# Two hybrid layers on one core: retention as full-array matmuls with zero-padded operands, the sum of the merged branches in SBUF, and longer times in the planner's yields

## The chip, the cores and the metric

The kernel runs on one core of a Trainium2 chip. The metric is the device time of one execution in microseconds (us). Five engines work side by side, each through its own instructions in order: PE (TensorE, matrix products), DVE (VectorE), ACT (ScalarE), POOL (GpSimd) and SP (SyncE, which here issues most of the DMA transfers). An instruction that needs the result of another engine waits, and whatever stands behind it on its engine waits with it. PE's clock has two levels, 1.2 and 2.4 GHz; the column PEclk of the profile is the granted clock as a share of the full one.

## The reference

Two blocks follow one another on a sequence of 512 positions of width 1024, in float32. The first (a gated recurrent mixer, a gated spatial mixer and a feed-forward part) is not touched. The second is two layers of this form:

```python
h = _rms(x) * norm1_g
proj = h @ w_in
aq, ak, av, rw, rq, rk, rv, rg, gates = _split(proj, IN_SIZES)
...
o_a = sliding_window_attention(aq, ak, av, attn_sinks) @ w_attn_o
o_b = rwkv7_time_mix(rw, ...) @ w_rwkv_o
o_c = retention(rq, rk, rv, rg) @ w_ret_o
g = jax.nn.sigmoid(gates).reshape(B, T, N_BRANCH, D)
mixed = g[:, :, 0] * o_a + g[:, :, 1] * o_b + g[:, :, 2] * o_c
x = x + mixed @ w_out
```

and then a feed-forward part with a residual. Each branch has 8 heads of 64 numbers. Retention goes over chunks of 128 positions, and carries a 64x64 state per head from one to the next:

```python
s = jnp.einsum('bnihd,bnjhd->bnhij', qc, kc) * dmat
inner = jnp.einsum('bnhij,bnjhe->bnihe', s, vc)
kv = jnp.einsum('bnjhd,bnjhe,hj->bnhde', kc, vc, zeta)
def step(R, kv_n):
    return R * chunk_decay[None, :, None, None] + kv_n, R
_, r_prev = lax.scan(step, jnp.zeros((B, H, d, d), jnp.float32), kv)
cross = jnp.einsum('bnihd,nbhde,hi->bnihe', qc, r_prev, xi)
```

## The kernel before

**Layout.** An activation is kept transposed: 8 tiles of 128 channels (partitions) by 512 positions. P is 128, T is 512, KT is 8.

**Dense products.** Each big product runs as three matmuls of 128x128 by 128x512 on the two halves (high and low) of both operands. The weights come in blocks. SP loads two blocks with one DMA of 512 KB (`raw`, line 89), ACT casts the high half of a block (`hl`, line 101), POOL subtracts it to get the low half (line 212, `hl<-raw,hl`), and PE works off 12 matmuls per block (line 151). Four `hl` buffers let ACT and POOL be up to three blocks ahead of PE. The products end in PSUM tiles `psd` (three), those of the small chains in `psr` (two pairs) and `psm` (one).

**A layer of the second block** (`layer`) has these stages, with their times in the profiled execution for the first and the second layer:
- the rwkv stage, 1060 to 1385 and 2100 to 2430 us: two chains `rwkv_pair`, of two head pairs each, with dense products in between;
- the attention stage, 1385 to about 1558 and 2430 to about 2602 us: two chains `attn_block` and the chain `ret` (retention), again with dense products in between;
- the rest of the dense products, to 1662 and 2705 us. They end with `projections(0)`, 8 blocks that multiply the attention output by `w_attn_o`;
- the `w_ret_o` stage, 8 blocks, to 1674 and 2717 us, and then `w_out` and the feed-forward part.

**What sets the order.** On PE the order of the program is kept (`manual_schedule`), and the function `weave` writes it. A chain is a generator. It issues its instructions up to a `yield` with a number: an estimate, in us of PE work, of how long the other engines need until the chain can go on. Until that much PE work (by the kernel's own counter `self.pe`) has been issued, `weave` takes steps of the other chains, or else of the dense products (`fmg`, three matmuls per step). A larger number therefore puts more dense matmuls between two parts of a chain. The order on the other engines and DMA queues is set by a scheduler, from the dependences and its own priorities.

**The sum of the branches.** Each of the three projections multiplies its product by a gate (`s`, loaded from DRAM into a tile `ld`; the DVE operation is on line 227) and adds it to a running sum. The sum lies in eight DRAM tiles `accd`. `projections(1)` stores it (`acc<-ld`). `projections(0)` and the `w_ret_o` stage load it (`ld<-acc`), add on DVE (line 212, `ld<-ld,ld`) and, in `projections(0)`, store it again.

**Retention** (`ret`). A chunk holds q and k as four tiles of two heads (64 partitions each). Scores take the 64 rows of one head as a 64x128 operand (in the profile `x,x`); the product with v is written in two halves of 64 output rows (`v,rs`), the product with the carried state `rr` in two halves of 64x64 (`rr,qx`).

**Names in the rwkv chain.** `AR,BK` are the two score groups of a pair, `SC` the masked scores that DVE makes of them; `kp` is a working tile (`wt`) that is copied from PSUM on line 1537, and `Zb` a tile whose copy from PSUM line 1513 makes and which a DMA (`solve`) rearranges.

## Time and profile before

| | us |
|---|---|
| median of three runs | 3144.87 |
| lowest, highest | 3140.88, 3152.83 |
| profiled execution | 3142.22 |
| its span | 3140.1 |
| PE busy | 2987.4 (95%) |
| mean granted clock of PE | 0.979 |

The span runs from the first to the last instruction of the core; 2.1 us of the execution lie around it. PE is busy for 95% of it, DVE for 47%, POOL for 44% and ACT for 36%.

### The profile page before, as it was taken

To read this page: it belongs to the slowest core of one execution; us is meant where nothing else is said; L and a number is where in the kernel's file an instruction comes from. 1 tells how busy PE (TensorE), PEld (TensorE's weight loads), DVE (VectorE), ACT (ScalarE), POOL (GpSimd) and SP (SyncE) were. 2 spreads that over 40 slices of the span, in tenths; PEclk is the share of its full clock that TensorE was granted. 3 is DMA by queue.
4 is the path that set the end of the run, shared out by engine and by line. 5 is a ranking of instruction groups with operands and counts; after the bars stand their busy time and mean duration, and the time that the engine had idled before them with its cause. 6 is when DMAs were issued, how large, how long until landed. Compare 5 with 4: busy or idle time off the path is not lost. (4 is left out here: it accounts for less than half of the span.)

```text
span 3140.1 us, 48643 instructions
## 1 busy us (share of the span) xinstructions
PE 2987.4 (95%) x19104; PEld 2406.1 (77%) x19104; DVE 1464.9 (47%) x2870; ACT 1120.9 (36%) x2059; POOL 1389.2 (44%) x1117
## 2 busy tenths in 40 slices
PE   6999999889999989998999999999999999999999
PEld 5787887678888767786777888877778778778887
DVE  6765457662324776636424222228574552432121
ACT  3544422243232433334423322334332453333232
POOL 3442444434444433242345555564233324465453
PEclk9999999999999999998999999999999999999999
DMA  5221346423333443342465323334333336632333
GB/s 205 75 80 56 108 141 225 170 68 97 98 94 98 136 111 96 94 132 86 141 202 174 101 93 95 100 132 127 91 100 118 112 95 186 227 99 92 97 94 94
DMA packets 206819, 372.32 MB, mean 119 GB/s; under 512 B 71040, under 2 KB 107136, under 8 KB 203520
## 3 DMA queue, kind: packets, MB, share of 16 engines
q1 hardware_dynamic: 185152, 365.78, 37.2%
q10 hardware_dynamic: 21440, 3.45, 0.6%
q8 instruction: 150, 2.46, 0.3%
q14 instruction: 77, 0.63, 0.1%
HBM read 323.02 MB, written 46.14 MB: 118 GB/s over the span
## 5 line engine op out<-in xcount | busy, mean ns | idle before, releaser
L212 POOL TENSOR_TENSOR hl<-raw,hl 128x512 fp32r<-128x512 f32 (+2 forms) x924 | 1194.6, 1297 | 1584.2 <-ACT hl L101 1442.7
L151 PE MATMUL psd<-u,hl 128*128 128x512 f32 (+1 forms) x7176 | 1720.2, 396 | 16.2 <-ACT u L231 3.5
L151 PEld LDWEIGHTS psd<-u,hl 128*128 128x128 f32 x7176 | 1334.1, 192 | 310.1 <-issue 12.1
L101 ACT CAST hl<-raw 128x512 fp32r<-128x512 f32 (+2 forms) x924 | 554.4, 604 | 1221.4 <-PE psd L151 934.6
L151 PE MATMUL psd<-hf,hl 128*128 128x512 f32 x1056 | 248.8, 396 | 0.0
L151 PEld LDWEIGHTS psd<-hf,hl 128*128 128x128 f32 x1056 | 197.8, 188 | 47.4
L151 PE MATMUL psd<-hl,hl 128*128 128x512 f32 x576 | 142.3, 406 | 13.3 <-DVE ld L227 13.3
L151 PEld LDWEIGHTS psd<-hl,hl 128*128 128x128 f32 x576 | 110.5, 194 | 43.5 <-issue 9.2
L212 DVE TENSOR_TENSOR s<-psd,rstd 128x512 f32<-128x512 f32 x88 | 60.5, 691 | 177.1 <-PE psd L151 153.7
L212 DVE TENSOR_TENSOR x<-x,psd 128x512 f32<-128x512 f32 x48 | 33.0, 687 | 235.9 <-PE psd L151 235.9
L227 DVE SCALAR_TENSOR_TENSOR hf<-s,hf 128x512 fp32r<-128x512 f32 x66 | 53.9, 817 | 155.7 <-ACT hf L139 155.5
L212 DVE TENSOR_TENSOR z<-psd,rstd 128x512 f32<-128x512 f32 x80 | 55.0, 688 | 137.3 <-PE psd L151 137.1
L151 PE MATMUL psd<-hl,u 128*128 128x512 f32 (+1 forms) x480 | 104.5, 366 | 2.2 <-DVE zq L227 1.9
L227 DVE SCALAR_TENSOR_TENSOR acc<-wada,cond,acc 128x256 f32<-128x256 f32 x152 | 99.3, 678 | 2.4
L212 DVE TENSOR_TENSOR raw<-raw,rows 128x512 f32<-128x512 f32 x60 | 57.5, 998 | 84.4 <-DMA raw<-in_wst 84.4
L151 PEld LDWEIGHTS psd<-hl,u 128*128 128x128 f32 x480 | 81.5, 190 | 18.3 <-DVE zq L227 2.0
L151 PE MATMUL psd<-mix,hl 128*128 128x512 f32 x384 | 89.4, 393 | 1.3 <-DVE ld L227 1.2
L139 ACT ACTIVATE hf<-s 128x512 fp32r<-128x512 f32 x66 | 41.7, 632 | 127.5 <-POOL s L212 116.7
L151 PEld LDWEIGHTS psd<-mix,hl 128*128 128x128 f32 x384 | 71.8, 188 | 18.7 <-DVE ld L227 3.0
L227 DVE SCALAR_TENSOR_TENSOR nt<-nt,nt 128x8 f32<-128x8 f32 (+3 forms) x330 | 78.6, 242 | 8.0
L227 DVE SCALAR_TENSOR_TENSOR s<-s,s 128x512 f32<-128x512 f32 x44 | 55.9, 1270 | 28.2 <-ACT s L139 28.0
L151 PE MATMUL psr<-hl,hf 128*128 128x512 f32 x264 | 66.9, 390 | 0.6 <-POOL hl L212 0.5
(374 smaller groups left out, 3230.7 us busy)
## 6 DMA issues: line engine op xcount, KB each, us to landing
raw<-in_wst SPq DMA_DIRECT2D x390, 512.0 KB, 3.6
wada<-in_wada SPq DMA_DIRECT2D x24, 1024.0 KB, 6.1
raw<-in_wst SPq DMA_DIRECT2D x32, 448.0 KB, 3.2
raw<-in_wst SPq DMA_DIRECT2D x32, 384.0 KB, 3.0
gd<-z SPq DMA_DIRECT2D x48, 256.0 KB, 4.2
ld<-gd SPq DMA_DIRECT2D x48, 256.0 KB, 3.9
acc<-ld SPq DMA_DIRECT2D x32, 256.0 KB, 3.5
ld<-acc SPq DMA_DIRECT2D x32, 256.0 KB, 3.7
```

Of the source, the lines that this page charges most:

```text
L101: self.nc.scalar.copy(h[:, 0, :w], t)
L139: return self.nc.scalar.activation(out, in_, getattr(AF, func), **k)
L151: return self.nc.tensor.matmul(out, lhsT, rhs, start=start, stop=stop, **k)
L212: return (eng or self.nc.vector).tensor_tensor(out, a, b, op=op)
L227: return self.nc.vector.scalar_tensor_tensor(out, a, s, b, op0=op0, op1=op1, **k)
```

## The change

**The sum of the branches.** `acc` is now one SBUF tile of 128 x 8 x 512, and the DRAM tiles are gone with their 32 stores and 32 loads of 256 KB. `projections(1)` writes `acc` with its DVE operation. `projections(0)` adds into it on POOL. The `w_ret_o` stage multiplies by the gate and adds `acc`, both on DVE.

**Retention.** Two tiles `qz` hold q with the other head's 64 partitions at zero; two tiles `rz` hold the carried state in the same way, and take turns over the chunks. Scores take all 128 rows of k and `qz`; the products with v and with the state are each one matmul with 128 columns of weights in place of two with 64. The state's update is two DVE multiplications of 64 partitions in place of one of 128. Per chunk ACT makes two copies of 64x512 into `qz`.

**Attention.** k is zero-padded in the same way, and its scores take all 128 rows. The loads of the mask and of the sinks stand earlier in the program.

**The planner.** Eight numbers in yields are larger, and the copy into `kp` goes from DVE to ACT.

```diff
         self.xd = [dt(f"xd{m}", [P, T]) for m in range(KT)]
-        self.accd = [dt(f"acc{m}", [P, T]) for m in range(KT)]
         self.gd = [[dt(f"gd{b}{m}", [P, T]) for m in range(KT)] for b in range(3)]
...
         return s
-
-    def merged(self, l, s, name, m, xs):
-
-        py = yield from self.fmg(name, l, range(m * P, (m + 1) * P), xs)
-        self.stt(s, s, 1.0, py, OP.add, OP.mult)
...
                     s = from_memory(self.gd[br][m])
+                    py = yield from self.fmg("w_rwkv_o_2" if br else "w_attn_o_2", l, range(m * P, (m + 1) * P), xs)
+                    o = acc[:, m] if br else s
+                    self.stt(o, s, 1.0, py, OP.add, OP.mult)
                     if br == 0:
-                        ld = from_memory(self.accd[m])
-                    yield from self.merged(l, s, "w_rwkv_o_2" if br else "w_attn_o_2", m, xs)
-                    if br == 0:
-                        self.add(s, s, ld)
-                    nc.sync.dma_start(self.accd[m], s)
+                        self.add(acc[:, m], acc[:, m], s, nc.gpsimd)
                     yield
...
             ahl, chl = new4(HP.pool, "a"), new4(HP.pool, "c")
+            acc = HP.pool.tile([P, KT, T], F, name=self.n("acc"), tag="acc")
             at = {}
...
             for m in range(KT):
-                s, ld = from_memory(self.gd[2][m]), from_memory(self.accd[m])
-                self.run(self.merged(l, s, "w_ret_o_2", m, cs))
-                self.add(s, s, ld)
+                s = from_memory(self.gd[2][m])
+                self.stt(s, s, 1.0, self.fm("w_ret_o_2", l, range(m * P, (m + 1) * P), cs), OP.add, OP.mult)
+                self.add(s, s, acc[:, m])
                 self.split_half(mix[m][:, 0], mix[m][:, 1], s)
...
         q = yp.tile([P, 4, T], F, name=self.n("q"), tag="yq")
-        k = yp.tile([P, T], F, name=self.n("k"), tag="yk")
+        k = yp.tile([P, 2, T], F, name=self.n("k"), tag="yk")
+        nc.gpsimd.memset(k, 0.0)
+        sw = self.cload(yp, "swmask")
+        sink = yp.tile([P, 8], F, name=self.n("sink"), tag="sink")
+        nc.sync.dma_start(sink, self.a["attn_sinks_2"][l:l + 1, :].broadcast_to((P, 8)))
         sq = yp.tile([P, 4, 10], F, name=self.n("sq"), tag="ysq")
...
         self.tm("w_in_2", l, range(I_AK, I_AK + 256), self.us, donek)
-        yield 7.0
+        yield 8.5
         r = self.rsqrt(yp, "ya", sq.rearrange("p t h -> p (t h)"), 1.0 / 64, RMS_EPS).rearrange("p (t h) -> p t h", h=10)
...
             self.tr(ps[:, t * P:(t + 1) * P], zk[:, t])
-        self.act(k, ps, "Copy", scale=self.v2("k_norm", l))
+        for kv in range(2):
+            h = slice(64 * kv, 64 * kv + 64)
+            self.act(k[h, kv], ps[h], "Copy", scale=self.v2("k_norm", l)[h])
         yield 1.0
...
             yield 0.8
-        sw = self.cload(yp, "swmask")
-        sink = yp.tile([P, 8], F, name=self.n("sink"), tag="sink")
-        nc.sync.dma_start(sink, self.a["attn_sinks_2"][l:l + 1, :].broadcast_to((P, 8)))
         env.update(q=q, k=k, vt=vt, sw=sw, sink=sink)
...
             for i in range(2):
-                self.mm(ps[:, i * 256:i * 256 + w], q[r, 2 * g + i, c], k[r, k0:k0 + w])
+                self.mm(ps[:, i * 256:i * 256 + w], q[:, 2 * g + i, c], k[:, kv, k0:k0 + w])
             self.add(s[:, 2 * g:2 * g + 2, :w], ps.rearrange("p (i s) -> p i s", s=256)[:, :, :w],
...
             self.act(s[:, h, :w], s[:, h, :w], "Copy", scale=mx[:, 3, h:h + 1])
-        yield 8.5
+        yield 10.0
         pt = yp.tile([P, 8, P], F, name=self.n("pt"), tag=f"ypt{kv}")
...
         x3 = xi.rearrange("p (j i) -> p j i", i=P)
-        r1 = None
-        bc = lambda t, n: t.rearrange("p (h o) -> p h o", o=1).broadcast_to((P, t.shape[1], n))
+
+        qz = [cp.tile([P, 4, P], F, name=self.n("qz"), tag=f"qz{e}") for e in range(2)]
+        rz = [cp.tile([P, 2, 4, 64], F, name=self.n("rz"), tag=f"rz{i}") for i in range(2)]
+        for t in qz + rz:
+            nc.gpsimd.memset(t, 0.0)
+        bc = lambda t, n: t.rearrange("p (h o) -> p h o", o=1).broadcast_to((t.shape[0], t.shape[1], n))
         for n in range(4):
...
             nc.sync.dma_start(g, self.rd["g"].rearrange("j p t -> p j t")[:, :, c])
-            r0 = r1
+            r0, r1 = rz[(n + 1) % 2], rz[n % 2]
             if n:
...
                 self.mul(kz, ps.rearrange("p (h d) -> p h d", d=64), bc(zeta, 64))
+            for e in range(2):
+                r = slice(64 * e, 64 * e + 64)
+                nc.scalar.copy(qz[e][r], q[r])
             yield 1.5
...
             for e in range(2):
-                r = slice(64 * e, 64 * e + 64)
                 ps = self.psum("r1")
                 for j in range(4):
-                    self.mm(ps[:, j * P:(j + 1) * P], k[r, j], q[r, j])
+                    self.mm(ps[:, j * P:(j + 1) * P], k[:, j], qz[e][:, j])
                 s.append(cp.tile([P, 4, P], F, name=self.n("rs"), tag=f"rs{e}"))
...
             for e in range(2):
-                r = slice(64 * e, 64 * e + 64)
                 po = self.psum("r1")
                 for j in range(4):
-                    for h in (slice(0, 64), slice(64, 128)):
-                        self.mm(po[h, j * 64:(j + 1) * 64], s[e][:, j, h], v[:, (2 * j + e) * 64:(2 * j + e) * 64 + 64], True, n == 0)
-                    for h in (slice(0, 64), slice(64, 128)) if n else ():
-                        self.mm(po[h, j * 64:(j + 1) * 64], qx[r, j, h], r0[r, j], False, True)
+                    self.mm(po[:, j * 64:(j + 1) * 64], s[e][:, j], v[:, (2 * j + e) * 64:(2 * j + e) * 64 + 64], True, n == 0)
+                    if n:
+                        self.mm(po[:, j * 64:(j + 1) * 64], qx[:, j], r0[:, e, j], False, True)
                 nc.scalar.copy(o[:, :, e], po[:, :256].rearrange("p (j d) -> p j d", d=64))
...
                     self.mm(ps[:, j * P:(j + 1) * P], kz[:, 2 * j:2 * j + 2].rearrange("p h d -> p (h d)"), v[:, j * P:(j + 1) * P])
-                r1 = cp.tile([P, 4, 64], F, name=self.n("rr"), tag="rr", bufs=2)
                 kv = ps.rearrange("p (j e d) -> p j e d", e=2, d=64)
-                if n:
-                    self.mul(r1, r0, bc(cd, 64))
                 for e in range(2):
...
                     if n:
-                        self.add(r1[r], r1[r], kv[r, :, e])
+                        self.mul(r1[r, e], r0[r, e], bc(cd[r], 64))
+                        self.add(r1[r, e], r1[r, e], kv[r, :, e])
                     else:
-                        nc.vector.tensor_copy(r1[r], kv[r, :, e])
+                        nc.vector.tensor_copy(r1[r, e], kv[r, :, e])
             o8 = o.rearrange("p j e d -> p (j e) d")
...
             self.mul(o8, o8, bc(rs, 64))
-            yield 10.5
+            yield 12.0
             ps = self.psum("r1")
...
         for h in range(2):
-            yield 2.2 if h else 11.0
+            yield 2.5 if h else 13.0
             pss = [psum() for _ in ER]
...
-        yield 1.9
+        yield 4.5
         UV = [tl(f"z{e}", (P, NC, 64)) for e in range(2)]
...
         wt = tl("kp", (P, NC, 64))
-        nc.vector.tensor_copy(wt, each(of(M1), of(xd)))
-        yield 1.4
+        nc.scalar.copy(wt, each(of(M1), of(xd)))
+        yield 2.0
         p2, p1 = each(of(zd), of(wt)), each(of(wt), of(zd))
...
         self.add(zd, p1, zd)
```

**The order in three places.** First PE in the first layer, third head pair: from the last matmul of its second score group (`AR,BK`) to the products `ident,z` that read the scores made of it. `u,hl` are dense matmuls. Before:

```order
L151 MATMUL psr_10757<-AR_10584,BK_10585 128x128
L151 MATMUL psd_10687<-u_8342,hl_10600 128x512 x3
L151 MATMUL psd_10687<-u_8342,hl_10619 128x512 x6
L151 MATMUL psr_10790<-ident,z_10391 64x64 x16
L151 MATMUL psr_10791<-ident,AR_10584 64x64 x16
```

And with the change:

```order
L151 MATMUL psr_10800<-AR_10612,BK_10613 128x128
L151 MATMUL psd_10715<-u_8342,hl_10647 128x512 x3
L151 MATMUL psd_10825<-u_8342,hl_10697 128x512 x3
L155 MATMUL psm_10834<-ident,b_10835 128x128 x4
L151 MATMUL psd_10825<-u_8342,hl_10697 128x512 x9
L151 MATMUL psd_10825<-u_8342,hl_10716 128x512 x3
L151 MATMUL psr_10883<-ident,z_10419 64x64 x16
```

The dense matmuls between the two went from 9 to 18, and a group of four transposes (`ident,b`) moved in between as well.

Second, the copy into `kp` of the first layer's first use. On DVE it stood, before the change, behind line 1513's copy into the `Zb` tile of the other chain:

```order
L212 TENSOR_TENSOR h_9686<-psd_9566,rstd_8753 128x512
L212 TENSOR_TENSOR tmp_9642<-Zb_9640,MB_9493 64x225
L1518 TENSOR_REDUCE Zb_9640<-tmp_9642 64x15
L227 SCALAR_TENSOR_TENSOR z_9689<-h_9686,omu,z_9689 128x512
L1513 COPY Zb_11208<-id_8774 64x256
L1537 COPY kp_9717<-psr_9718 128x512
L212 TENSOR_TENSOR tE_9474<-psr_9742,tE_9474 128x512
```

With the change it stands on ACT, between the two `solve` transfers that ACT issues:

```order
L1510 COPY tsq_9692<-psr_9675 128x512
L1518 COPY Xb_9695<-Zb_9694 64x256
L1521 DMA solve_8397<-Zb_9694 64x16x16
L1536 COPY kp_9740<-psr_9741 128x512
L101 CAST hl_9762<-raw_9562 128x512
L1521 DMA solve_8398<-Xb_9695 64x16x16
```

It left DVE's queue, where a copy that waits for a transfer was ahead of it, for ACT's, where a copy into `Xb` and the issue of a transfer are ahead of it.

Third, POOL in the first layer's `projections(0)`, with the change. Before, the rows here are the weight splits (`hl<-raw,hl`) alone:

```order
L212 TENSOR_TENSOR hl_14217<-raw_14144,hl_14217 128x512
L212 TENSOR_TENSOR hl_14239<-raw_14181,hl_14239 128x512
L212 TENSOR_TENSOR acc_12190<-acc_12190,ld_14214 128x512
L212 TENSOR_TENSOR hl_14259<-raw_14181,hl_14259 128x512
L212 TENSOR_TENSOR acc_12190<-acc_12190,ld_14236 128x512
L212 TENSOR_TENSOR hl_14281<-raw_14220,hl_14281 128x512
```

Every second row is now an add into `acc`. The first add is that of the first of the eight blocks (weights `hl_14158`), and the split behind it (`hl_14259`) is that of the sixth.

## Rows read from the trace of the kernel before

**Rows 1.** Windows: length, busy PE, PEld, DVE, ACT, POOL, then PEclk, DMA share, GB/s.
```profile
1060.00:1385.00 325.00, 308.17 (x3337) 244.91 (x3336) 202.41 (x427) 114.62 (x201) 125.11 (x110) 0.97 0.39 110
1385.00:1600.00 215.00, 202.04 (x1229) 160.62 (x1228) 102.77 (x240) 94.15 (x231) 73.24 (x59) 0.96 0.42 126
...
2100.00:2430.00 330.00, 312.40 (x3348) 248.28 (x3347) 202.18 (x426) 115.90 (x204) 124.56 (x107) 0.97 0.38 108
2430.00:2600.00 170.00, 157.87 (x1042) 125.49 (x1041) 94.60 (x228) 81.44 (x210) 54.38 (x44) 0.96 0.36 109
```

**Rows 2.** Waits of PE: line, releaser, us in total, times, longest.
```profile
PE psr L151 <- DVE SC L212: 18.5, 8, 3.1
PE psd L151 <- DVE ld L227: 14.4, 12, 2.9
...
PE psr L151 <- DVE kp L1537: 8.3, 2, 5.0
```

**Rows 3.** PE's timeline, last 16 blocks ahead of `w_out`: start, us, [idle before].
```profile
1618.69 19.75 PE L151 MATMUL psd<-hl,hl 128*128 128x512 f32 x84
...
1674.19 4.27 PE L151 MATMUL psd<-mix,hl 128*128 128x512 f32 x16
...
2663.12 22.55 PE L151 MATMUL psd<-hl,hl 128*128 128x512 f32 x96
...
2717.24 1.56 PE L151 MATMUL psd<-mix,hl 128*128 128x512 f32 x6
```

**Rows 4.** PE's timeline, dense matmuls of the second layer, without a wait.
```profile
2619.17 44.12 PE L151 MATMUL psd<-u,hl 128*128 128x512 f32 x192
```

**Rows 5.** The chain that ended last, second layer's `projections(0)`: start, us, step.
```profile
2668.72 2.88 DMA acc<-ld
2671.61 4.12 DMA ld<-acc
```

**Rows 6.** Lines, POOL and DVE: group xcount | busy us, mean ns | idle before.
```profile
L212 POOL TENSOR_TENSOR hl<-raw,hl 128x512 fp32r<-128x512 f32 (+2 forms) x924 | 1194.6, 1297 | 1584.2 <-ACT hl L101 1442.7
...
L212 DVE TENSOR_TENSOR ld<-ld,ld 128x512 f32<-128x512 f32 x32 | 28.0, 875 | 34.6 <-DMA ld<-acc 34.3
```

**Rows 7.** PE's timeline, waits of the first layer's rwkv stage, in brackets.
```profile
1110.96 2.58 PE L151 MATMUL psr<-AR,BK 64*128 64x128 f32 x16 [1.73 <-DVE SC L212]
...
1130.41 1.75 PE L151 MATMUL psr<-AR,BK 64*128 64x128 f32 x16 [1.55 <-DVE SC L212]
...
1158.62 1.30 PE L151 MATMUL psr<-kp,tkk 64*64 64x64 f32 x32 [3.30 <-DVE kp L1537]
...
1250.66 0.97 PE L151 MATMUL psr<-ident,z 64*64 64x64 f32 x26 [3.07 <-DVE SC L212]
...
1274.08 1.93 PE L151 MATMUL psr<-AR,BK 64*128 64x128 f32 x16 [2.73 <-DVE SC L212]
```

**Rows 8.** Timeline of ACT and DVE ahead of the `kp` copy, first layer.
```profile
1154.26 0.65 ACT L1519 COPY Xb<-Zb 64x256 f32<-64x256 f32 x1
...
1157.68 0.28 DVE L1513 COPY Zb<-id 64x256 f32<-64x256 f32 x1 [2.74 <-DMA solve<-Zb]
```

**Rows 9.** Windows of 5 us behind the wait for `kp`, columns as in rows 1.
```profile
1160.00:1165.00 5.00, 5.00 (x73) 4.10 (x69) 2.29 (x4) 1.34 (x2) 1.15 (x1) 0.71 0.37 82
```

**Rows 10.** Lines, PE: the retention scores, all chunks of both layers.
```profile
L151 PE MATMUL psr<-x,x 64*128 64x128 f32 x128 | 14.7, 281 | 0.0
```

**Rows 11.** PE's timeline, small products; the last two are of retention's first chunk.
```profile
1142.10 2.00 PE L151 MATMUL psr<-DI,BK 64*128 64x64 f32 x32
...
1417.15 1.15 PE L151 MATMUL psr<-v,rs 128*64 128x64 f32 x32
...
1418.23 1.16 PE L151 MATMUL psm<-v,kz 128*128 128x128 f32 x8
```

**Rows 12.** The chain that ended last: retention's products with v and state, one later chunk.
```profile
2506.65 4.24 PE psr L151 x64
```

**Rows 13.** Timeline of ACT, the first weight cast of the attention stage, first layer.
```profile
1390.12 1.14 ACT L101 CAST hl<-raw 128x512 fp32r<-128x512 f32 x2 [8.72 <-DMA raw<-in_wst]
```

## The prediction

> **What bounds the kernel now.** I read the windows first. In the stages of the second block PE is busy nearly all the time, at nearly the full clock: idle are 16.8 and 17.6 us of the two rwkv stages (325.00 − 308.17, 330.00 − 312.40) and 13.0 and 12.1 us of the two attention stages [rows 1]. So PE sets the end, and a change is worth what it takes from PE's idle time, from its half-clock stretches, or from the work itself. The waits of PE say what that idle time is for: masked scores from DVE (SC, 18.5 us in 8 waits), PSUM tiles that the gating on DVE frees late (ld, 14.4 us in 12), the copy into kp (8.3 us in 2) [rows 2]. The change touches all three.
>
> **The sum of the branches: −20 us.** A block of 12 dense matmuls takes 12 × 44.12 / 192 = 2.76 us when nothing waits [rows 4], so the 16 blocks ahead of w_out are worth 44.1 us. They take 1674.19 − 1618.69 = 55.5 us in the first layer and 2717.24 − 2663.12 = 54.1 us in the second [rows 3], so 21.4 us are lost, the 14.4 us of waits for ld [rows 2] and the half clock behind them. The chain shows why: a store of the sum takes 2.88 us, and the load of it, which cannot start before, 4.12 us [rows 5]. DVE's add waits for that load (34.3 us in all [rows 6]), the next gating stands behind the add in DVE's order, and PE waits for the PSUM tile that this gating frees. Without stores and loads that cause is gone. What comes instead must fit into 2.76 us a block. POOL, in projections(0): a split of 1.30 us and an add of the same shape, which is the same operation with another sign, 1.30 more [rows 6], together 2.6. The first add stands four splits before it can matter (the split behind it is that of the sixth block), so its lag is covered; if the pair takes longer than 2.76, each block loses the difference. DVE, in the w_ret_o stage: the add at 0.88 us [rows 6], and two gating operations whose cost I estimate as at most that of the add, again 2.6 in all. Both fit narrowly; I leave 1.4 of the 21.4 us, and take −20. Bounds: −21.4, and −10 (POOL at 1.7 us per operation, a third above its mean, would give back 0.64 us for each of 16 blocks).
>
> **The padded operands: −2 us.** The profile shows each float32 product as two records, so a retention chunk's products with v and state go from 64 records to 32, the first chunk's from 32 to 16. Before they take 4.24 us [rows 12] and 1.15 us [rows 11], per layer 1.15 + 3 × 4.24 = 13.9 us. After, a layer has 16 + 3 × 32 = 112 records with 128 columns of weights. No row shows this form on 64 columns. The nearest: 64x128 operands, 32 records in 2.00 us (0.063 each), with two heads' rows alternating; retention's scores, 14.7 us for 128 records (0.115 each) [rows 10], one head after the other; and 128x128 operands, 8 records in 1.16 us (0.145 each) [rows 11]. That gives 7.0, 12.9 or 16.2 us a layer. I take 0.115, since the new products come one behind the other too: −1.0 a layer, −2 in all, between −14 and +5. The scores themselves keep their number of matmuls, and so cost what they cost. In the attention the same holds.
>
> The Trainium skill speaks against this part: "TensorE: Matmul & The Clock Gate", Part 3 (packing small matmuls), says that products in different row groups of the array run at the same time, which padding would undo. By that rule the scores' 14.7 us would have been shared by two heads, and padding would double them: −2 would become +12.7. The row does not bear it out: the two heads' products stand one group behind the other in the program, and 0.115 us a record is near the 0.145 of a full array, not half of it.
>
> **The yields and the kp copy: −20 us.** A dense matmul costs PE 0.23 us [rows 4] wherever it stands, so moving it ahead of a wait shortens that wait by 0.23. In the first layer's rwkv stage the waits are 1.73, 1.55, 3.30, 3.07 and 2.73 us [rows 7]; the order on PE says what each gets:
> - Ahead of the first (a second score group that waits for SC): 6 more, −1.4. Ahead of the second: 12 more, all of its 1.55 is covered.
> - kp: 3 more, and the copy leaves DVE. On DVE it stood behind a copy that waited 2.74 us for a transfer until 1157.68; on ACT it stands behind a copy at 1154.26 of 0.65 us [rows 8] and the issue of a transfer. PE started at 1158.62 [rows 7], and could start some 2 us earlier: −2.0 of 3.30. The rest of the wait stays, since the input of the copy is no earlier. It now delays one weight cast on ACT by its own length, under 1 us, against blocks of weights worth 2.76 us each that are ready ahead.
> - ident,z after the second score group of the third pair: 9 more matmuls and four transposes, at 0.23 and at least 0.145 [rows 11], −2.7 of 3.07.
> - The wait of 2.73: the matmuls between the score groups go from 12 to 6, since the other chain's time came earlier. That makes it longer by 1.4.
>
> Sum −6.2. Behind a long wait the clock falls: the 5 us after the kp wait have 0.71 of it [rows 9], 0.29 × 5 = 1.45 us lost. Three of the five waits become too short for that, an assumption that only the trace of the changed kernel can show: −4.4. That makes −10.6, and I take −10 a layer, since the second layer has the same order and slightly longer waits [rows 2]. Bounds: −4 for both (only kp), and −34 of idle time with −15 of clock (ten such stretches), −49 in all.
>
> **The attention stage: −1 us.** By its end 30 more dense matmuls have been placed, but the long waits there are behind DVE's softmax, which gets no shorter. Some waits gain 6 matmuls (−1.4), others lose as many. At its start SP issues three small loads before the weights, and the first cast had already waited 8.72 us for them [rows 13]. POOL has five memsets, at most 1.3 us each for a 128x512 tile (the price of a split of that shape), some 7.8 us with the double width of k, in the lead of three blocks, 8.3 us. ACT has two more copies a chunk, DVE one more multiplication. I take −1; bounds −12 (half of the idle time) and +9 (one more such wait, shared by the layers).
>
> **Sum.** −20 − 2 − 20 − 1 = −43: the profiled execution's 3142.2 becomes 3099. It lies 2.65 us under the median of the runs, which I add: 3102.
>
> **The rivals.**
> - *Waits only move.* The chains are bound by DVE, and a longer yield only lets DVE's own work for the added dense blocks come first. For it: the wait of 2.73 gets fewer matmuls. Against: it is the order on PE that puts them between. Then −20 − 2 − 4 = −26: 3119.
> - *The waits vanish, and with them the half clock.* −21.4 − 2 − 49 = −72: 3073. Against: kp's input is no earlier, and one wait has less cover.
> - *POOL becomes the bound in projections(0).* At 1.7 us per operation, −10 on the first term: 3112.
> - *Row groups lost.* +14.7 as worked out above: 3117.
> - *Slower: SP holds back the weights in retention.* In the order of the changed kernel SP's load of a next chunk's q waits for ACT's copies into qz, and weight loads stand behind it. If PE then waits in each of four chunks of both layers as long as the cast did [rows 13], 8 × 8.72 = 70 us are added: 3172. From 5.4 us a chunk it eats the gain, from 7.3 the kernel is slower by over 0.5%. Against: q's buffer waited for PE before, and ACT is far from full [rows 1].
>
> **How the numbers follow.** Chances: 3102 0.50 (its own range 3085 to 3117), waits move 0.20, waits vanish 0.17, POOL 0.05, row groups 0.04, SP 0.04. The range has to leave out no more than 0.2: from 3072, the case of vanishing waits, to 3128, the case of moving waits with the +9 of the attention stage. About 0.5%, 15.7 us, is what a measurement of this kernel can tell from no change; that is 3129 and less for faster. Faster: all but SP, less some of the moving waits and of the upper bounds, 0.88; same 0.08; slower 0.04.
>
> **What would show it.** No acc transfers, and 16 blocks ahead of w_out in about 45 us. The wait for ld gone from PE's list, that for SC at about half, for kp at 4 us or less. Retention's products at 3.5 to 3.8 us a later chunk, the scores still at about 0.115 us a record. Wrong would be: POOL's add as PE's releaser, retention's scores at twice their time, a wait for raw in the attention stage on ACT above 9 us, or SC's waits undiminished.

## The result and the profile after

The changed kernel takes 3112.12 us (median of four runs, 3110.09 to 3113.77), beside 3144.22 for the kernel before (also the median of four; the 3144.87 ahead of the prediction is that of three); the ratio is 0.9893, with a 95% interval from 0.9873 to 0.9914. So it is 32 us faster, where 43 were predicted. The time lies in the range, within the likeliest case's own range, and between that case (3102) and the one in which waits only move (3119).

PE's list of waits after, which answers to [rows 2] (line, releaser, us in total, times, longest):

```profile
PE psr L151 <- DVE SC L212: 15.7, 6, 3.2
PE psr L155 <- ACT s L139: 14.3, 2, 7.4
...
PE psr L151 <- ACT kp L1536: 3.4, 2, 2.0
...
PE psd L151 <- DVE ld L227: 2.8, 2, 1.4
```

The wait for `ld` has gone from 14.4 us to 2.8, that for `kp` from 8.3 to 3.4. The wait for `SC`, predicted at about half, went only from 18.5 to 15.7. And two long waits for `ACT s` are new, 14.3 us, where the kernel before has ten short ones, 7.3 us in all. These are for the scaled scores of the attention's softmax.

PE's timeline shows where the time came from. The first two rows are each layer's first dense matmul; then come the 16 blocks ahead of `w_out`, which answer to [rows 3]:

```profile
1068.96 1.42 PE L151 MATMUL psd<-u,hl 128*128 128x512 f32 x5 [1.46 <-DVE h L212]
...
2099.31 0.97 PE L151 MATMUL psd<-u,hl 128*128 128x512 f32 x3 [1.54 <-DVE h L212]
...
1618.03 44.97 PE L151 MATMUL psd<-hl,hl 128*128 128x512 f32 x192
1662.84 1.54 PE L151 MATMUL psd<-mix,hl 128*128 128x512 f32 x6
...
2643.59 44.97 PE L151 MATMUL psd<-hl,hl 128*128 128x512 f32 x192
2688.40 1.54 PE L151 MATMUL psd<-mix,hl 128*128 128x512 f32 x6
```

In the kernel before, the first two rows were these:

```profile
1062.84 1.42 PE L151 MATMUL psd<-u,hl 128*128 128x512 f32 x5 [1.46 <-DVE h L212]
2108.39 0.97 PE L151 MATMUL psd<-u,hl 128*128 128x512 f32 x3 [1.54 <-DVE h L212]
```

With them the span can be cut at the same matmuls in both traces:

| stretch | before, us | after, us | difference |
|---|---|---|---|
| first block, up to the first layer's first dense matmul | 1062.8 | 1069.0 | +6.1 |
| rwkv and attention stages, first layer | 555.9 | 549.1 | -6.8 |
| 16 blocks, first layer | 55.5 | 44.8 | -10.7 |
| `w_out` and feed-forward, first layer | 434.2 | 436.5 | +2.3 |
| rwkv and attention stages, second layer | 554.7 | 544.3 | -10.4 |
| 16 blocks, second layer | 54.1 | 44.8 | -9.3 |
| rest | 422.9 | 423.6 | +0.7 |

The sum is -28.1, the difference of the two spans (3140.1 and 3112.0). The 6.1 us in the first block belong to this execution: the first block's instructions stand in the same order on every engine, and in the profiled executions of two versions with the same first block, below, its end is at 1062.18 (`e6_pooladd`) and 1058.37 us (`e4_sc`).

The windows below go, in each layer, from its first dense matmul to `w_out`; first the kernel before, then the changed one (columns as in [rows 1]):

```profile
1062.84:1674.19 611.35, 576.47 (x4825) 457.65 (x4826) 331.55 (x701) 227.22 (x462) 226.29 (x190) 0.97 0.44 131
2108.39:2717.24 608.85, 573.92 (x4824) 456.53 (x4825) 332.85 (x699) 226.09 (x461) 223.88 (x186) 0.97 0.44 129
...
1068.96:1662.84 593.88, 565.27 (x4713) 457.94 (x4714) 333.50 (x694) 234.31 (x476) 237.77 (x203) 0.98 0.42 122
2099.31:2688.40 589.09, 564.76 (x4712) 457.37 (x4713) 331.67 (x692) 233.38 (x475) 235.19 (x199) 0.98 0.42 121
```

In the two layers PE is idle for 69.8 us before and for 52.9 after (length less busy time). The half clock costs 39.2 us before and 27.2 after; this is (1 - granted clock) x length, summed over windows of 1 us. The idle time fell by 9.7 us in the rwkv stages and by 13.3 in the 16 blocks, and rose by 6.1 in the attention stages.

### The profile page after: what moved, and what is told of

Same layout as the page of the kernel before. It is cut to its first block, busy times and chain, and to the rows that moved or that the text cites. A ratio compares the mean times of both kernels' runs of the same rounds, so it can differ in the third digit from the quotient of the medians.

```text
span 3112.0 us, 48091 instructions
## 1 busy us (share of the span) xinstructions
PE 2969.0 (95%) x18880; PEld 2409.3 (77%) x18880; DVE 1467.9 (47%) x2850; ACT 1133.9 (36%) x2085; POOL 1408.7 (45%) x1143
## 3 DMA queue, kind: packets, MB, share of 16 engines
q1 hardware_dynamic: 175936, 348.99, 35.9%
## 5 line engine op out<-in xcount | busy, mean ns | idle before, releaser
L227 DVE SCALAR_TENSOR_TENSOR s<-s,s 128x512 f32<-128x512 f32 x44 | 55.6, 1263 | 28.3 <-ACT s L139 28.1
```

What stands on the lines that cost most here:

```text
L227: return self.nc.vector.scalar_tensor_tensor(out, a, s, b, op0=op0, op1=op1, **k)
```

## The experiments

**The three parts by themselves.** Three kernels take the kernel before and make one part of the change each.

```diff
 e1_acc: accd, its loads and stores removed, acc in SBUF; nothing else
+            acc = HP.pool.tile([P, KT, T], F, name=self.n("acc"), tag="acc")
 e2_yields: the eight numbers and the engine of the kp copy; nothing else
-        yield 1.9
+        yield 4.5
...
-        nc.vector.tensor_copy(wt, each(of(M1), of(xd)))
+        nc.scalar.copy(wt, each(of(M1), of(xd)))
 e3_pad: qz, rz and the padded k; nothing else
+                    self.mm(ps[:, j * P:(j + 1) * P], k[:, j], qz[e][:, j])
```

> The kernel before with the sum of the branches in SBUF alone. Theory: the 16 blocks ahead of w_out take about 45 us in each layer instead of 55.5 and 54.1, and w_out then meets a wait of about 1.4 us a layer, so 17 to 20 us less than before: about 3125 to 3128. Rival 1: the store and the load only stood in front of another limit (DVE), and half or less of the 20 us appears: above 3134. Rival 2: the 6 us by which block 1 was longer in the profile of the changed kernel come from the DRAM tiles that are gone and from where that puts the others; then block 1 ends 6 us later here too. If they belong to that execution alone, block 1 is as before.

> The kernel before with the larger yields and the kp copy on ACT alone. Theory: what the rwkv stages gained in the changed kernel (4.2 and 8.9 us by the position of the same matmuls in both traces) comes from here, -13; the attention stages add or take little; the waits for SC stay at about 15 us since the matmuls between the two score groups went from 15 and 12 to 12. Total -10 to -14: 3130 to 3134. Rival: these yields were only of use with the padded operands, whose PE estimate is shorter; then the attention stages lose here and the total is nearer to 0.

> The kernel before with the padded operands in retention and attention alone, yields as before. Theory: retention's products with v and state take 3.5 us a later chunk instead of 4.2 and the first one 1.8 instead of 1.15, the scores are as before or 0.1 us a chunk longer: -2 to -3 on PE. Since the counter of the planner now counts half of what it counted for these products, the chains of the attention stage come elsewhere, and their waits may move by some us either way: 3138 to 3146. Rival: row groups ran together before, then the scores are longer by some 15 us in all.

| | median, us | before beside it | ratio, 95% interval |
|---|---|---|---|
| `e1_acc` | 3126.19 | 3144.68 | 0.9944, 0.9928 to 0.9960 |
| `e2_yields` | 3133.99 | 3144.68 | 0.9962, 0.9947 to 0.9978 |
| `e3_pad` | 3151.44 | 3144.68 | 1.0020, 1.0004 to 1.0036 |

The first two came as expected: -18.5 and -10.7 us. The padding alone is 6.8 us slower (1 to 11 by its interval), outside what was expected. The three add up to -22.4, and the change gave -32.1, so some 10 us come only with two parts together.

**Which two parts.** The changed kernel with the sum back in DRAM has padding and yields alone.

```diff
 e13_noacc, against the changed kernel
-            acc = HP.pool.tile([P, KT, T], F, name=self.n("acc"), tag="acc")
+        self.accd = [dt(f"acc{m}", [P, T]) for m in range(KT)]
 (with its loads and stores)
```

> The changed kernel with the sum of the branches back in DRAM, so padding and yields together without the first part. The three parts alone gave -18.5, -10.7 and +6.8, in all -22.4, and the change gave -32.1: some 10 us are due to two parts being together. Theory: padding and yields work together (in the attention stages, where each alone lost 5 to 8 us and both together gained 3), so this run is some 14 us faster than before: 3128 to 3133. Rival: the sum in SBUF is what works together with one of them; then this run is at the sum of the two alone, -4: 3138 to 3143.

It took 3127.95 us beside 3147.12 before (0.9940, 0.9920 to 0.9959): -19.2, where the two alone would give -3.9. So it is padding and yields that work together. Whether the sum in SBUF is quite independent of them can't be told: -18.5 and -19.2 make -37.7, and the change gave -32.1, between -27 and -40 by its interval.

What they gain together can be read from the traces, one profiled execution of each version. The table holds, for the two layers from their first dense matmul to `w_out`, the length, PE's idle time and what the half clock costs, as above; the lower rows belong to runs described below.

| | length, us | PE idle, us | half clock, us |
|---|---|---|---|
| before | 1220.2 | 69.8 | 39.2 |
| `e2_yields` | 1208.7 | 65.7 | 34.0 |
| `e3_pad` | 1228.8 | 84.2 | 35.7 |
| `e13_noacc` | 1197.1 | 65.0 | 25.5 |
| changed kernel | 1183.0 | 52.9 | 27.2 |
| `e4_sc` | 1177.5 | 54.1 | 22.1 |
| `e5_attn` | 1178.5 | 49.6 | 23.8 |
| `e9_sc_attn` | 1166.5 | 48.9 | 13.6 |
| `e14_nopad` | 1196.0 | 46.2 | 46.1 |
| `e11_more` | 1193.9 | 63.2 | 32.4 |

Padding alone costs PE 14 us of idle time. With the longer yields this cost is gone: 65.0 us with padding and 65.7 without. That is most of what the two gain together; the rest is the half clock. (The execution of `e13_noacc` is the shortest of its four, so the table shows some 5 us more than the medians.)

**Why the padding alone costs.** The first idea was the planner's counter. In `mm`, a padded product with 128 columns of weights is counted at 0.22 us, and the two with 64 that it replaces at 0.11 together, so the products of a later chunk count 3.5 us and not 1.7; then fewer dense matmuls are placed. (The expectation of `e3_pad` had this the wrong way round.)

```diff
 e10_count, against e3_pad
+                    t0 = self.pe
                     self.mm(po[:, j * 64:(j + 1) * 64], s[e][:, j], v...
...
+                    self.pe = t0 + (4 if n else 2) * 64 * 0.00083
```

> The padded operands alone (as in the run of that name), but with the planner's counter raised for retention's padded products by what it was raised before the change (1.7 us a later chunk, where it now adds 3.5; the chip takes 3.5 to 4.2). An earlier expectation said that the counter now counts half: it counts double, so fewer dense matmuls are put between the parts of the chains. Theory: the padding alone cost 6.8 us only for that reason; with the old count the matmuls between the parts are those of before, and 3 to 8 us come back against that run: 3143 to 3148 beside 3144 before, or less. Rival: the padding itself costs (ACT's copies into qz ahead of the exponentials, DVE's extra multiplication), and the time stays within 2 us of the padding alone, 3149 to 3154.

The theory fell: 3154.45 us beside 3146.14 (1.0024, 1.0013 to 1.0035). With the old count the dense matmuls between the parts are those of the kernel before, and the padding costs 8.3 us all the same. Up to 1513 us the attention stage gains 2.6 us on the kernel before, by the same matmuls in both traces; then one wait takes 5 back. PE's row of it, and DVE's rows ahead of it:

```profile
1522.52 1.98 PE L151 MATMUL psr<-pt,vt 128*64 128x128 f32 x16 [2.98 <-DVE pt L1245]
...
1517.69 1.13 DVE L224 TENSOR_SCALAR nt<-rms 128x8 f32<-128x8 f32 x1
...
1521.78 0.68 DVE L1245 COPY pt<-psr 128x512 f32<-128x512 f32 x1
```

PE reached its transposes earlier, but the copy of their result (`pt`) now stands behind retention's row of small operations in DVE's order, three of which took 1.13 to 1.19 us each. That accounts for the wait in this stretch; the second layer lost 4 to 5 us at the same place (by the same matmuls, +8.2 us ahead of it and +12.9 behind it). From the end of the rwkv stage to `w_out` the first layer came out even (304.9 us beside 305.4) and the second 7.0 us longer (308.6 beside 301.6), so this one place explains the larger part of the second layer's loss and not all of it. Not tried was another order on DVE alone.

**What the padding is worth in the fastest version** (`e9_sc_attn`, below). The same without padding:

```diff
 e14_nopad: the kernel before with acc in SBUF, the yields and the kp copy of the change, and
+            yield 6.5 if h else 13.0
+        yield 16.0
```

> The fastest version so far (both longer yields, 6.5 and 16) without the padded operands. Theory: padding gives PE 1 to 3 us in all and costs waits only where DVE comes late, so with these yields the two are close: 3088 to 3096 beside 3091. Rival 1: padding costs 7 us here as it did alone, 3082 to 3086. Rival 2: it works together with the yields here too, and without it the attention stages lose 10 us or more: above 3099.

It took 3110.43 us beside 3147.12 before, and `e9_sc_attn` 3091.35 beside 3144.30: without padding 19 us are missing, the second rival. Here, other than in the change itself, idle time is not the reason. Below are the attention stages of both: first the two layers of `e14_nopad`, then those of `e9_sc_attn` (columns as in [rows 1]).

```profile
1391.00:1621.00 230.00, 219.59 (x1282) 176.09 (x1281) 106.97 (x243) 96.57 (x236) 80.64 (x65) 0.93 0.41 120
2406.00:2641.00 235.00, 224.75 (x1307) 179.30 (x1306) 113.01 (x256) 96.36 (x236) 80.69 (x65) 0.91 0.40 116
```

```profile
1386.00:1606.00 220.00, 206.77 (x1171) 172.67 (x1170) 107.54 (x246) 101.88 (x246) 83.81 (x70) 0.98 0.44 126
2404.00:2623.00 219.00, 207.48 (x1169) 173.06 (x1169) 107.91 (x244) 101.88 (x246) 83.94 (x71) 0.98 0.44 128
```

Without padding PE is idle for 10.4 and 10.3 us, with it for 13.2 and 11.5; but the granted clock is 0.93 and 0.91 against 0.98 and 0.98. (1 - 0.93) x 230 + (1 - 0.91) x 235 = 37 us are lost to the half clock without padding, 0.02 x 439 = 9 us with it. This execution of `e14_nopad` was the longest of its four, 3123.77 us, so a usual one loses less: in the three others the mean granted clock of the whole run was 0.979 to 0.981, in the four of `e9_sc_attn` 0.984 to 0.986, on average 62 and 46 us lost. That is 16 of the 19 us. One place where the clock falls in the one and not in the other is retention's second chunk. `e14_nopad`, PE's timeline and windows:

```profile
1478.78 0.48 PE L151 MATMUL psr<-rr,qx 64*64 64x64 f32 x4
1479.19 2.08 PE L151 MATMUL psm<-v,kz 128*128 128x128 f32 x8
1481.19 6.63 PE L151 MATMUL psr<-k,q 64*128 64x256 f32 x16
...
1480.00:1485.00 5.00, 5.00 (x16) 4.10 (x16) 2.21 (x4) 0.34 (x1) 1.46 (x2) 0.50 0.41 118
1485.00:1490.00 5.00, 5.00 (x12) 3.31 (x11) 4.69 (x13) 0.47 (x2) 1.08 (x1) 0.50 0.04 13
```

And `e9_sc_attn`, the windows with the same chunk:

```profile
1460.00:1470.00 10.00, 10.00 (x82) 8.92 (x80) 4.94 (x9) 3.16 (x7) 3.12 (x3) 1.00 0.53 160
1470.00:1480.00 10.00, 9.35 (x51) 7.87 (x50) 8.26 (x23) 2.28 (x8) 2.57 (x2) 1.00 0.25 66
```

In `e14_nopad` PE is busy 10.00 of 10 us, and yet the clock stands at 0.50, the 1.2 GHz level: it fell at the end of the 64-row and 64-column products (the eight `v,kz` behind them already take 2.08 us, in the changed kernel 1.11) and stays there over the next scores, 16 records in 6.63 us; with the padded products it stays at 1.00, the 2.4 GHz level, even with 0.65 us of idle time. The Trainium skill, "TensorE: Matmul & The Clock Gate", Part 1, puts the low clock down to idle time and the high one to a busy engine; this stretch differs from that, and the measurement decides: an engine that was busy with small tiles lost the clock too.

It is not the only such place. By windows of 0.5 us the half clock costs 35.9 us in the attention stages of this execution: 15.4 in five stretches behind waits, and 20.5 in five that had no idle time in the 5 us ahead of them. Each of the latter begins at the end of the `v,rs` and `rr,qx` products of a later chunk. So do the only three others in the traces of the two layers up to `w_out`: one in the kernel before (1.7 us) and two in `e1_acc` (5.1 us). `e2_yields`, with the same products, has none, and neither has any of the ten padded versions. So these products did not cost the clock each time; what decides it was not tested.

**The score groups.** The wait for `SC` did not shrink as predicted. Its place in the changed kernel, PE's timeline:

```profile
1111.41 1.16 PE L151 MATMUL psr<-AR,BK 64*128 64x128 f32 x16
1112.51 3.04 PE L151 MATMUL psd<-u,hl 128*128 128x512 f32 x12
1118.71 1.54 PE L151 MATMUL psr<-AR,BK 64*128 64x128 f32 x14 [3.17 <-DVE SC L212]
```

DVE's rows for `SC` at this place, in the kernel before (where the first group ended at 1105.6) and in the changed one (1112.6):

```profile
1110.24 1.26 DVE L212 TENSOR_TENSOR SC<-psr,qm 128x512 f32<-128x512 f32 x2
...
1117.37 0.69 DVE L212 TENSOR_TENSOR AR<-z,tP 128x512 f32<-128x512 f32 x1 [0.69 <-ACT tP L139]
1117.97 1.28 DVE L212 TENSOR_TENSOR SC<-psr,qm 128x512 f32<-128x512 f32 x2
```

The table has the four pairs of the first layer. The lag is the time from the end of the first score group to the end of DVE's first multiplication for `SC`; the work is what PE does between the two groups; the wait is PE's, ahead of the second group.

| pair | lag before, after | work before, after | wait before, after |
|---|---|---|---|
| first | 5.3, 6.1 | 3.6, 3.0 | 1.73, 3.17 |
| second | 4.3, 6.0 | 2.8, 3.5 | 1.55, 2.50 |
| third | 2.2, 5.6 | 3.0, 3.0 | 0, 2.67 |
| fourth | 5.6, 3.8 | 3.0, 3.7 | 2.73, 0 |

In all eight cases the wait is the lag less the work, where that is more than nothing. The work fell in the first pair only, from 15 dense matmuls to 12. What changed more is the lag, and that is DVE's order: a multiplication for `SC` takes 0.67 us, but in the first three pairs of the changed kernel it stands behind other rows, and DVE pauses for at most 0.7 us between. They are a row of small `nt` operations in the first pair, the other chain's operations around `solve` in the second, and in the third an `nt` row that stood behind `SC` before. Some of the small operations are slow. Of the 288 `nt` operations on 128x8 in the changed kernel's trace 37 took over 0.9 us, the others 0.17 on average; each of the 37 began while an operation ran on POOL and ended within 0.03 us of the end of one.

More work between the groups would cover a long lag. One yield more makes the test:

```diff
 e4_sc, against the changed kernel
-            yield 2.5 if h else 13.0
+            yield 6.5 if h else 13.0
```

> The changed kernel with the yield ahead of the second score group of the rwkv chain at 6.5 in place of 2.5. Theory: a wait is covered only by matmuls between the event that starts DVE's work and the waiting matmul, here between the first score group and the second; these were 15, 9 and 12 before and are 12, 6 and 6 in the changed kernel, and become about 15 to 30 now. The waits for SC (15.7 us) should fall to under 4, and with them some of the half-clock stretches: -12 to -20 against the changed kernel, about 3092 to 3100. Rival: DVE is behind with the evacuation of the added dense blocks, so SC comes later by as much; the waits stay above 10 us and the time within 5 us of the changed kernel's.

It took 3099.84 us, 12.3 less than the changed kernel (0.9858 of the kernel before, 0.9844 to 0.9873). The waits between the score groups are gone, but not all for `SC`, and a new one came (`BKt`):

```profile
PE psr L151 <- ACT BKt L1498: 11.7, 4, 4.1
PE psr L151 <- DVE SC L212: 9.3, 4, 3.4
...
1119.31 0.97 PE L151 MATMUL psr<-ident,z 64*64 64x64 f32 x26 [3.43 <-DVE SC L212]
```

The wait has moved one step on, to `ident,z` behind the second group: 24 dense matmuls stand between the two now, but `SC` comes 9.1 us behind the group. So the expected 4 us of `SC` were missed, while the time came as expected. (The expectation's 9 matmuls in the second pair are 3 in the trace, beside products of the other chain.)

The time did not come by way of the idle time, which is 54.1 us in the two layers beside 52.9 in the changed kernel. Of the 17.7 us between the two spans 10.6 lie in the first block, which the edit leaves alone, and 1.6 between the layers; 5.4 lie in the layers, and the half clock makes up 5.1 of them. So these two executions show some 7 of the 12.3 us that lie between the medians.

**The new wait in the attention.** In the changed kernel, PE and then ACT:

```profile
1470.52 1.89 PE L151 MATMUL psr<-k,q 128*128 128x256 f32 x8
...
1477.32 1.64 PE L151 MATMUL psd<-u,hl 128*128 128x512 f32 x6
1485.91 2.29 PE L155 MATMUL psr<-ident,s 128*128 128x128 f32 x8 [6.95 <-ACT s L139]
```

```profile
1483.58 1.31 ACT L139 ACTIVATE s<-s,mx 128x256 f32<-128x256 f32 x3 [1.77 <-DVE mx L1229]
```

From the end of the scores, at 1472.4, to the transposes DVE and ACT need 13.5 us, and the order gave PE some 6.6 us of work in between.

```diff
 e5_attn, against the changed kernel
-        yield 10.0
+        yield 16.0
 e9_sc_attn: this and the yield of e4_sc
```

> The changed kernel with the yield of attn_block ahead of the transposes at 16 in place of 10. Theory: the one wait of 7 us in each layer for the scaled scores of the second query block (ACT s, 14.3 us in 2) is there because only some 6.6 us of PE work stand between the scores and the transposes while DVE and ACT need 13; with 21 to 39 dense matmuls between them it goes, -10 to -16 with the clock behind it. Rival: DVE and ACT are the bound of this stage and retention's chain is then the one that waits; the wait takes another name and the time stays within 5 us.

> Both longer yields, 6.5 ahead of the second score group and 16 ahead of the transposes, in the changed kernel. Theory: the two waits are in different stages and the gains add: the sum of the two runs apart, about -22 to -34, 3078 to 3090. Rival: dense matmuls moved ahead in the rwkv stage are missing in the attention stage, and the gains overlap: less than two thirds of the sum.

`e5_attn` took 3100.97 us, 11.2 less than the changed kernel, and no wait for `ACT s` is left among the larger ones; that for DVE's `s` grew from 7.8 to 12.0 us, and 7.4 us of waits for `pt` are new. In the two layers the idle time fell by 3.3 us and the half clock by 3.4, so here too the traces show only a part of the difference. Both yields together gave 3091.35 us (0.9832 of the kernel before, 0.9816 to 0.9849), 20.8 less than the changed kernel, of 23.4 by the sum. In the two layers this version has only 4.0 us less of idle time than the changed kernel, but none of its waits there is longer than 3.6 us, where the longest was 7.4, and the half clock costs 13.6 us in place of 27.2. It is the fastest version found. Two more yields did not help:

```diff
 e11_more, against e9_sc_attn
-        yield 4.5
+        yield 8.0
...
             nc.scalar.copy(BKt[e], c8(pk[e]))
-        yield 2.0
+        yield 5.0
```

> Both longer yields (6.5 and 16), and two more in the rwkv chain: ahead of ident,z 8.0 in place of 4.5, and behind the copies into BKt 5.0 in place of 2.0. Theory: in the run with both longer yields PE still waits 9.8 us for SC ahead of ident,z and 9.8 us for BKt; with 9 to 15 more dense matmuls there both go to under 4 us in all, -10 to -18 against that run, 3073 to 3082. Rival: the dense matmuls that are moved ahead are missing behind (the attention stage starts with fewer), or DVE and ACT have become the bound of the rwkv stage; the time stays within 5 us of that run, 3087 to 3096.

It took 3118.66 us, 27 more. The first rival was right in direction, and far too small. PE at the end of the first layer's rwkv stage:

```profile
1377.67 2.34 PE L151 MATMUL psd<-u,hl 128*128 128x512 f32 x9
1385.17 1.97 PE L151 MATMUL psr<-ident,ta 64*64 64x64 f32 x32 [5.16 <-DVE ta L212]
```

In the changed kernel 60 dense matmuls stand ahead of these products; here 9 are left, since the rest was placed earlier. This wait is 10.3 us in the two layers, but the waits for `SC` and `BKt` that the yields were meant for fell by about as much, and the rwkv stages came out 3.8 us longer. The loss, 23.7 us, is in the attention stages, where retention and attention meet in another order: 15.3 us more of idle time, and 16.2 more for the half clock (idle time at the half clock counts in both). Which chain is to blame there was not tested.

**The engine of the kp copy.** Back on DVE, with all else as changed:

```diff
 e8_kpdve, against the changed kernel
-        nc.scalar.copy(wt, each(of(M1), of(xd)))
+        nc.vector.tensor_copy(wt, each(of(M1), of(xd)))
```

> The changed kernel with the kp copy back on DVE, yields as in the changed kernel. Theory: the copy now stands behind DVE's row of small products and sums of the other chain in place of ACT's queue, and PE's wait for kp grows from 2.0 and 1.4 us to 3 to 5 us a layer: +3 to +7 with the clock. Rival: the longer yields alone have shortened the wait, the copy's engine does not matter: within 2 us.

3109.75 us (0.9889, 0.9875 to 0.9904): 2.4 us less than the changed kernel, so the theory falls, and the rival holds but for 0.4 us. With the new yields the copy stands ahead of the copy into `Zb` in DVE's order as well. PE's waits for `kp` are 4.8 us with DVE, 3.4 with ACT and 8.3 before, so it was mostly the new place in the order that shortened them, not the engine.

**The wait that is left at w_out.** DVE in the changed kernel's `w_ret_o` stage:

```profile
1659.41 0.68 DVE L227 SCALAR_TENSOR_TENSOR ld<-ld,psd 128x512 f32<-128x512 f32 x1
...
1661.62 0.69 DVE L227 SCALAR_TENSOR_TENSOR mix<-ld,mix 128x512 fp32r<-128x512 f32 x1 [0.70 <-ACT mix L139]
1662.23 0.68 DVE L227 SCALAR_TENSOR_TENSOR ld<-ld,psd 128x512 f32<-128x512 f32 x1
```

```diff
 e6_pooladd, against the changed kernel
-                self.add(s, s, acc[:, m])
+                self.add(s, s, acc[:, m], nc.gpsimd)
```

> The changed kernel with the add of acc in the w_ret_o stage on POOL in place of DVE. Theory: the wait of 1.41 and 1.43 us ahead of the second group of w_out's matmuls is DVE's backlog of three operations a block (DVE ld), so it goes: -2 to -3 against the changed kernel. Rival: the last tile of mix is late anyway since POOL's add is longer and stands behind a split; then the wait takes another name and the time stays or grows by 1 to 2 us.

3121.79 us, 9.7 more: the rival, and more than it said. In DVE's order the operation that makes `mix` stands ahead of the next block's gating, and waits for the add and ACT's copy:

```profile
2687.09 0.68 DVE L227 SCALAR_TENSOR_TENSOR ld<-ld,psd 128x512 f32<-128x512 f32 x1
2689.97 0.69 DVE L227 SCALAR_TENSOR_TENSOR mix<-ld,mix 128x512 fp32r<-128x512 f32 x1 [2.20 <-ACT mix L139]
2690.57 0.68 DVE L227 SCALAR_TENSOR_TENSOR ld<-ld,psd 128x512 f32<-128x512 f32 x1
```

So one block's turn on DVE is a chain, gating, add, copy, `mix`. It takes 2.8 us in the changed kernel (from 1659.41 to the next gating 2.82 later), and 3.5 to 3.9 with the add on POOL. DVE's busy time alone is not what counts there.

## Why the prediction was nearly right

- **The sum of the branches: -20, right.** The 16 blocks take 44.8 us in each layer, so -20.0, and -18.5 by `e1_acc`. The 1.4 us left open came as waits of 1.41 and 1.43 us at `w_out`, by DVE's chain; POOL's pair of split and add did not make PE wait.
- **The padded operands: -2, the wrong kind of answer.** As PE time the term was right: the products take 1.73 us in the first chunk and 3.52 in a later one, so 12.3 us a layer, where 12.9 was predicted. PE's timeline after, and the group of the scores (busy us, mean ns):

```profile
1430.94 1.90 PE L151 MATMUL psr<-v,rs 128*128 128x64 f32 x16
1432.67 1.11 PE L151 MATMUL psm<-v,kz 128*128 128x128 f32 x8
...
1523.35 0.33 PE L151 MATMUL psr<-v,rs 128*128 128x64 f32 x2
...
1526.87 1.11 PE L151 MATMUL psm<-v,kz 128*128 128x128 f32 x8
...
L151 PE MATMUL psr<-qz,x 128*128 128x128 f32 x128 | 15.8, 276 | 0.0
```

  The scores take 15.8 us, where [rows 10] had 14.7: they did not double, since one head's products stood behind the other's and there was little overlap to lose (see the last section). One reading was wrong: the `DI,BK` row of [rows 11] has 64x64 operands and not 64x128, so the bound of -14 rested on a form that is further off than it says. And the term held only PE time. Padding also moves the waits (+6.8 alone, +8.3 with the same order of dense matmuls) and keeps up the clock (most of the 19 us in the fastest version). Neither was a term of the sum, nor a rival.
- **The yields: -20, too much.** Alone they gave -10.7. The step that failed is "ahead of the first 6 more, ahead of the second 12 more". It takes the added matmuls off the waits as if `SC` came at the same time as before. But `SC` can't come before PE has done the first score group, which moved back too, and in DVE's order it came later still: the lag grew by 0.8, 1.7 and 3.4 us in the first three pairs. Predicted were waits of 0.3 and 0 us, measured 3.17 and 2.50. The third pair has a new one of 2.67 us, and the wait of 2.73 that was to grow by 1.4 is gone: the matmuls between fell to 6, but products of the other chain came in their place, and the lag fell by 1.8. `e4_sc` shows that work between the groups takes their wait away, and that most of it then comes back one step on. One count came true: `ident,z` with 9 to 18 matmuls lost all of its 3.07 us. For `kp`, 3.30 became 2.01 us and 4.99 became 1.40, near what was said, but mostly by the place in the order and not the engine.
- **The attention stage: -1.** "Some gain 6 matmuls, others lose as many" was no estimate of size. One wait grew from 1.60 to 6.95 us in the first layer, since a pair of chains met in another order; `e5_attn` took it away, for smaller ones elsewhere.
- **The rivals.** None came true by itself. That waits only move, since DVE's own work comes first, was true of `SC`, in the change and in `e4_sc`. SP held nothing back: the largest wait of a weight cast for `raw` in the attention stages is 3.74 us.
- **Luck.** That -32 came so near -43 is in part luck. Alone the yields gave about half of what was forecast and the padding cost 6.8 us; the 15 us by which the two together beat their sum stood in no term.

## What to carry to other kernels

A wait is the late engine's lag less the work between the event that starts the lag and the waiting instruction. Work that is placed ahead of both moves both. So count in the order of the program between these two, and not from the start of the stage; and read in the late engine's own order what stands ahead of the instruction that is waited for, since a new plan can lengthen that too.

Nearly the same idle time went with half the loss to the half clock where the waits were shorter: the fastest version has 4 us less of idle time in the two layers than the changed kernel, and loses 14 us less to the half clock. That the length of the waits is the reason was not tested by itself.

Numbers of a planner interact with each other and with the length of what they plan around: parts of a change that lose 7 us or gain 11 alone gave 19 together, and a yield that took 12 us off had a neighbour that put 27 back. Measure such numbers in the version in which they are to stay.

## What the runs showed of the hardware

The granted clock of PE fell to 1.2 GHz in a stretch without any idle time by the profile (10.00 us busy of 10.00), behind products on 64 rows and 64 columns, and in seven more such stretches of the four traces without padding. In the ten traces with these products zero-padded to the whole array there is none. Padding that wins little on the products themselves (13.9 us a layer became 12.3) can be worth more through the clock of the dense matmuls behind them.

Products on different row groups ran together where they follow one another directly. In the rwkv chain's score groups two heads alternate, product by product; in retention's, of the same form, all four products of one head stand ahead of those of the other. Both below are from the kernel before, at the full clock; then comes a place where the attention's scores (rows 64 to 127) met retention's (rows 0 to 63):

```profile
1124.90 1.11 PE L151 MATMUL psr<-AR,BK 64*128 64x128 f32 x16
...
1413.24 1.71 PE L151 MATMUL psr<-x,x 64*128 64x128 f32 x16
...
1457.32 0.48 PE L151 MATMUL psr<-k,q 64*128 64x256 f32 x1 [0.19 <-DVE s L212]
1457.33 0.48 PE L151 MATMUL psr<-x,x 64*128 64x128 f32 x2
```

The last two start 0.01 us apart, and the 16 records of `AR,BK` start two by two, 0.01 us apart as well; of those of `x,x` only three pairs do, where the heads meet. This agrees with the rule of the Trainium skill, "TensorE: Matmul & The Clock Gate", Part 3, that products in different row groups run at the same time. So the padding lost little by it, but it was not the only way: with retention's heads alternating, the eight chunks' scores would take PE some 8 x (1.71 - 1.11) = 5 us less, as an estimate from these two rows. That was not tried.
